# Hybrid trunk kernel: recurrence outputs loaded at the first product of the second double unit, pooled-channel forms tied to places in the product order

## Chip, cores and metric

The kernel runs on one core of one Trainium2 chip, as one launch. The metric is the device time of a launch in microseconds (us).

## What is computed

One layer of a streaming encoder on x of 2048 frames by 1024 channels, in fp32. Two branches read one input projection; each is projected to 1024 channels and merged under sigmoid gates; a gated feed-forward network follows. Cut to what matters here:

```python
xn = rmsnorm(x, norm1_g[l])
z = xn @ w_in[l]
u_pool, zq, zf, zi, zo, zg = jnp.split(z, splits, axis=-1)
gates = jax.nn.sigmoid(zg + b_gate[l]).reshape(B, S, N_BRANCHES, D_MODEL)
ya = pool_mixer(u_pool, pool_w[l], pool_scale[l]) @ w_pa[l]     # pool_mixer: 512 channels
yb = hgrn2_mixer(zq, zf, zi, zo, lower_bounds[l], hgrn_norm_g[l]) @ w_pb[l]   # 4 heads of 128
merged = gates[:, :, 0] * ya + gates[:, :, 1] * yb
x = x + merged @ w_o[l]
x = x + conv_glu_ffn(rmsnorm(x, norm2_g[l]), w_up[l], conv_w[l], conv_b[l], w_down[l])
```

`hgrn2_mixer` is a gated linear recurrence over chunks of frames, with an RMS norm and an output gate behind it; `pool_mixer` subtracts each token from trailing-window means and mixes the channels within four groups.

## The kernel before

**Blocks.** The frames are worked in two blocks of 1024, each of two halves `hf` of 512 (a tile is 128 channels by 512 frames). Names carry the number of the half: `mf0...` is of the first block, `mf2...` of the second.

**Products.** A fp32 operand is split into a high part (a cast on ACT) and a low part (a subtraction on DVE), and each product is three matmuls: high by high, high by low, low by high. `split` does it for activations (L659 ACT, L660 DVE, tiles `...h` and `...l`); the weight stream does it for weights (L231 ACT, L232 DVE, tiles `ops`), which it loads raw on SP's queue (L197, 8 raw buffers and a ring of 6 converted ones). Every matmul of these stages is recorded at L148.

**Units.** The larger projections use a Strassen-Winograd scheme with seven products in the order P1, P6, P5, P7, P2, P4, P3. Each product takes one form of the activations: P1 takes B11, P6 T2, P5 T1, P7 T3, P2 B21, P4 T4 and P3 B22, where T1 to T4 are sums and differences of the quarter blocks. The results go to three banks of PSUM: X (P1, P2), Z (P6, P7, P4) and V (P5, P3). Before a bank is used again, ACT copies X out (`e`, L1200) and DVE combines Z into `u` (L1202 after P6, L1206 after P7), so that P7 waits for the first and P4 for the second.

**Stages of a block's mixer**, in PE's order:
1. the input projections; the last unit is gr_7 (gate channels). The recurrence (pv, po: L1112, L1128, L1130; its transposes pt, L1147) runs among them, and its outputs are stored to memory (`od`) per half and head;
2. pa, the projection of the pooled channels, in two double units (d = 0 is pa_0 and pa_1, d = 1 is pa_2 and pa_3). A product of a double unit is 12 matmuls, and takes one weight. Its results are `ya` (L1161, L1572, L1577, L1579 on DVE, then L1580, the multiplication by the gate `gl`, on POOL);
3. pb, the projection of the recurrence's outputs, 16 chains of 12 matmuls on the split outputs `oTs`;
4. wo, the output projection (`wo_P`), whose forms `yf` are made in pb.

The feed-forward stages come after, with both blocks.

**What sets the order.** The program is written in one order for all engines, and a scheduler moves instructions within an engine's queue by their dependencies and estimated times. Side work is written as generators (`Task`): the kernel counts matmuls, every 6 matmuls are a tick, and at each tick every live task runs to its next `yield n` (n ticks until it goes on). `in_turn(ins)` ties an instruction behind the newest matmul in the scheduler's order; it adds no semaphore.

Two such tasks are touched. `pa_task` fetches the eight pooled tiles (`mx`, L964) at P1 of gr_7 and then makes the forms of pa, one form tile per tick: `minus` (L1486) makes a difference on DVE, L1513 the negated B22 on ACT, and `split` the two parts. Where a product of pa finds its form missing, the loop steps the task until it is there. `halves_task` does the recurrence's outputs from P5 of the second double unit on: it loads one (`oT<-od`, L964, on SP's queue), splits it, waits one tick, and goes to the next. POOL also adds up weights for the stream (L446, tiles `raw` and `w135s`).

Of the kernel before, what the change touches and what calls it, by code (L numbers as in the profile page):

```python
# [14 lines left out]
AF = mybir.ActivationFunctionType  # L15
ALU = mybir.AluOpType
# [6 lines left out]
HEADS = 4  # L23
# [31 lines left out]
PROJ = (("fq", 0), ("g", 0), ("u", 0), ("fq", 1), ("g", 1), ("g", 2), ("fq", 2), ("g", 3),  # L55
        ("u", 1), ("g", 4), ("fq", 3), ("g", 5), ("g", 6), ("g", 7))
# [9 lines left out]
WARM = 24, 5  # L66
GO_IO = (("P2", 1), ("P2", 0))
G_POOL = 4
O_AT, O_LAG = 4, 1
FIN_WAIT = 4  # L70
AHEAD = 3
ADD_LAG = 3
# [9 lines left out]
def tile_trunk(  # L82
# [16 lines left out]
    pe, act, dve, pool, sp = nc.tensor, nc.scalar, nc.vector, nc.gpsimd, nc.sync  # L99
# [9 lines left out]
    def slot(name, cols=TB, dt=F32):  # L109
        return slots.tile([P, cols], dt, tag="s", name=name, padded_shape=[P, 528])  # L110
# [4 lines left out]
    def f32(ap):  # L115
        return ap.bitcast(F32)
# [158 lines left out]
    def in_turn(ins):  # L275

        tc.add_manual_dep(ins.ins, count[1].ins.name, mybir.DependencyInfo(
            mybir.DependencyClass.NoSync, mybir.DependencyReason.SCHED_ONLY), reason="in turn")
# [235 lines left out]
    prep, quiet = [], [False]  # L514
# [136 lines left out]
    last_split = [None]  # L651

    def split(src, name, on_pool=False):
        hi = slot(name + "h", TB, F32R)
        lo = slot(name + "l", TB, F32R)
        if on_pool:
            up = pool.tensor_scalar(hi, src, 1.0, 0.0, ALU.mult, ALU.add)
        else:
            up = act.copy(hi, src)  # L659
        low = dve.tensor_tensor(lo, src, f32(hi), ALU.subtract)  # L660
        last_split[0] = up, low
        return hi, lo
# [299 lines left out]
    def fetch(d, name, eng=sp):  # L962
        t = slot(name)
        eng.dma_start(t, d)  # L964
        return t
# [407 lines left out]
    def mixer(b0, forms, late):  # L1373
# [4 lines left out]
        md, od, gd = {}, {}, {}  # L1378
# [74 lines left out]
                gd[s, m, hf] = spill(t, f"gd{b0 + hf}_{s}_{m}")  # L1453
            return emit

        def halves_task(src, keys, dst, name, lag=1):
            for hf in range(2):
                for g in keys:
                    while (b0 + hf, g) not in src:
                        yield 1  # L1460
                    t = fetch(src[b0 + hf, g], f"{name}{b0 + hf}_{g}")
                    dst[hf, g] = split(t, f"{name}s{b0 + hf}_{g}")
                    yield lag

        gates = {}

        def gate(s, m, hf):
            if (s, m, hf) not in gates:
                gates[s, m, hf] = fetch(gd[s, m, hf], f"gl{b0 + hf}_{s}_{m}")
            return gates[s, m, hf]  # L1470

        pf = {k: [] for k in ("B11", "B21", "B22", "T1", "T2", "T3", "T4")}

        def pa_task():
            t = {}
            for hf, g in ((0, 0), (0, 1), (1, 0), (1, 2), (1, 1), (1, 3), (0, 2), (0, 3)):
                while (b0 + hf, g) not in md:
                    yield 1
                t[hf, g] = fetch(md[b0 + hf, g], f"mx{b0 + hf}_{g}")

            def form(key, j, x):
                pf[key].append(split(x, f"mf{b0}{key}{j}"))

            def minus(key, j, x0, x1, eng=dve):
                x = slot(f"mf{b0}_{key}{j}")
                eng.tensor_tensor(x, x0, x1, ALU.subtract)  # L1486
                return x

            for j in range(2):
                form("B11", j, t[0, j])  # L1490
                yield 1
            t1, t2 = [], []
            for j in range(2):
                t1.append(minus("t1", j, t[1, j], t[0, j]))
                t2.append(minus("t2", j, t[1, j + 2], t1[j]))
                form("T2", j, t2[j])
                yield 1
            t3 = [minus("t3", j, t[1, j], t[1, j + 2], pool) for j in range(2)]
            for j in range(2):
                form("T1", j, t1[j])  # L1500
                yield 1
            for j in range(2):
                form("T3", j, t3[j])
                yield 1
            for j in range(2):
                form("B21", j, t[0, j + 2])
                t4 = minus("t4", j, t[0, j + 2], t2[j])
                yield 1
                form("T4", j, t4)
                yield 1  # L1510
            for j in range(2):
                x = slot(f"mf{b0}_b22{j}")
                act.activation(x, t[1, j + 2], AF.Copy, scale=-1.0)  # L1513
                form("B22", j, x)
                yield 1

        emits = {"fq": emit_fq, "u": emit_u, "g": emit_g}
        oT = {}
        for n, (kind, i) in enumerate(PROJ):
            if (kind, i) == ("u", 0):  # L1520
                held["w"] = stream.get("pw")
            u = Unit(f"{kind[0]}r{b0}_{i}", "in", emits[kind](i))
            for p in ORDER:
                u.multiply(p, forms, late)
                u.after(p)
                if n == len(PROJ) - 1 and p == "P1":
                    quiet[0] = True
                    mtask = Task(pa_task())

        def branch(key, s, xs, evac, each):  # L1530
            ws = {}
# [34 lines left out]
        def emit_a(i):  # L1566
            def emit(s, hf, a, ps):
                m = i + KD // 2 * s
                t = y[m, hf] = slot(f"ya{b0 + hf}_{m}")
                g = gate(0, m, hf)  # L1570
                if a is None:
                    dve.tensor_tensor(t, g, ps, ALU.mult)  # L1572
                    return
                if not hf:
                    value(t, a, ps)
                elif s:
                    dve.scalar_tensor_tensor(t, ps, -1.0, a[0], ALU.mult, ALU.subtract)  # L1577
                else:
                    dve.tensor_tensor(t, ps, a[0], ALU.subtract)  # L1579
                pool.tensor_tensor(t, t, g, ALU.mult)  # L1580
            return emit

        def evac_b(m, hf, g, ps):
            gated(g, hf, g, ps)
            dve.tensor_tensor(y[m, hf], y[m, hf], g, ALU.add)
            if m >= KD // 2 and hf:
                k = m - KD // 2
                two = {(h, r): y[k + r * (KD // 2), h] for h in range(2) for r in range(2)}
                add_forms(two, yf, k, f"yf{b0}", eng=dve)

        otask = []
        for d in range(2):
            units = [Unit(f"pa{b0}_{2 * d + e}", "pa", emit_a(2 * d + e)) for e in range(2)]
            for p in ORDER:
                if (d, p) == (1, "P5"):
                    otask.append(Task(halves_task(od, range(HEADS), oT, "oT", O_LAG)))
                for s_, hf in {"P6": ((1, 1),), "P5": ((0, 0),), "P7": ((1, 0),),
                               "P2": ((0, 1),)}.get(p, ()):
                    for e in range(2):
                        gate(0, 2 * d + e + KD // 2 * s_, hf)  # L1600
                while len(pf[FORM[p]]) < 2:
                    mtask.step()
                w = stream.get("pa")
                for e in range(2):
                    units[e].products(p, pf, pf[FORM[p]], w[:, :, e * 256 : e * 256 + 256])
                    units[e].after(p)
                stream.used(1)
# [340 lines left out]
```

## Time and profile before

| | |
|---|---|
| time, three runs | 2541.48, 2546.94 (median), 2548.03 us |
| profiled execution | 2544.34 us, its span 2542.6 us |
| granted TensorE clock, mean | 0.996 |
| first block, gr_7's first matmul to pa_2's | 419.42 to 474.03 us |
| first block, pa_2's first matmul to wo's | 474.03 to 549.40 us |
| second block, the same two stretches | 1683.32 to 1734.00 and 1734.00 to 1805.46 us |

Times in views are from the start of the span. A row of a timeline has the start, the duration, the engine, the line, the operation, output and inputs; in brackets stands how long the engine had been idle before it and what ended that. A window row has its bounds, its length, the busy time of the engine asked for (and its instructions), the granted clock, the busy share of the DMA engines and GB/s.

### The profile page before, as it was taken

To read this page: it belongs to the slowest core of one execution; us is meant where nothing else is said; L and a number is where in the kernel's file an instruction comes from. 1 tells how busy PE (TensorE), PEld (TensorE's weight loads), DVE (VectorE), ACT (ScalarE), POOL (GpSimd) and SP (SyncE) were. 2 spreads that over 40 slices of the span, in tenths; PEclk is the share of its full clock that TensorE was granted. 3 is DMA by queue.
4 is the path that set the end of the run, shared out by engine and by line. 5 is a ranking of instruction groups with operands and counts; after the bars stand their busy time and mean duration, and the time that the engine had idled before them with its cause. 6 is when DMAs were issued, how large, how long until landed. Compare 5 with 4: busy or idle time off the path is not lost.

```text
span 2542.6 us, 35725 instructions
## 1 busy us (share of the span) xinstructions
PE 2505.1 (99%) x11460; PEld 2049.3 (81%) x11460; DVE 1989.2 (78%) x3528; ACT 1215.1 (48%) x2286; POOL 804.2 (32%) x1171
## 2 busy tenths in 40 slices
PE   9999999899999999999999999998999999999998
PEld 7888888678888888888888888886788888888887
DVE  7787878688999777885596777786979888778755
ACT  6534443325555544554554444543355545445534
POOL 4343453312344334451320202123023432325410
PEclk9999999999999999999999999999999999999999
DMA  8877786587898879997344343446453554446952
GB/s 271 269 199 224 207 227 213 166 256 228 211 250 237 232 230 237 266 363 243 120 150 151 111 130 110 142 137 219 142 166 102 155 153 141 147 140 237 326 164 98
DMA packets 252332, 493.76 MB, mean 194 GB/s; under 512 B 26544, under 2 KB 43056, under 8 KB 251824
## 3 DMA queue, kind: packets, MB, share of 16 engines
q1 hardware_dynamic: 184512, 313.60, 39.0%
q0 software_dynamic: 42656, 112.74, 17.5%
q10 hardware_dynamic: 24976, 65.13, 7.5%
q8 instruction: 91, 1.49, 0.2%
q14 instruction: 97, 0.79, 0.1%
HBM read 381.79 MB, written 187.17 MB: 224 GB/s over the span
## 4 chain that ended last, share of the span: by engine, by line
PE 91%; DVE 3%; DMA 2%; issue 1%; ACT 1%; POOL 1%; SPq 0%; ACTq 0%; POOLq 0%; DVEq 0%
PE dn_P L148 16%; PE up_Z L148 14%; PE up_X L148 10%; PE up_V L148 10%; PE gr_Z L148 5%; PE wo_P L148 5%; PE gr_X L148 3%; PE gr_V L148 3%; PE io_Z L148 3%; PE fr_Z L148 3%; PE pb L148 2%; PE io_V L148 2%; PE fr_V L148 2%; PE fr_X L148 2%; PE pl L1029 2%; PE ur_Z L148 1%
## 5 line engine op out<-in xcount | busy, mean ns | idle before, releaser
L231 ACT CAST ops<-raw 128x512 fp32r<-128x512 f32 x794 | 490.3, 620 | 840.6 <-PE dn_P L148 180.1
L232 DVE TENSOR_TENSOR ops<-raw,ops 128x512 fp32r<-128x512 f32 x794 | 590.5, 747 | 233.8 <-ACT ops L231 228.9
L1681 DVE SCALAR_TENSOR_TENSOR e<-h,cols,e 128x512 f32<-128x512 f32 x176 | 143.3, 818 | 30.5 <-ACT e L1679 23.9
L1679 ACT ACTIVATE e<-h,cols 128x512 f32<-128x512 f32 x176 | 142.2, 814 | 25.3 <-DVE h L1162 18.4
L1684 DVE SCALAR_TENSOR_TENSOR e<-h,cols,e 128x512 f32<-128x512 f32 x176 | 133.9, 770 | 2.5
L964 POOL DMA_DIRECT2D g_P<-dg_P x154 | 83.7, 545 | 160.6 <-PE dn_P L148 111.0
L1275 POOL TENSOR_TENSOR gf_P<-e,e 128x512 f32<-128x512 f32 x44 | 61.1, 1390 | 150.7 <-DVE e L1690 96.1
L446 POOL TENSOR_TENSOR raw<-raw,raw 128x512 f32<-128x512 f32 x36 | 51.2, 1423 | 150.5 <-DVE ops L232 136.5
L1275 POOL TENSOR_TENSOR gf_P<-gf_P,e 128x512 f32<-128x512 f32 x44 | 59.2, 1346 | 71.6 <-DVE e L1690 71.1
L1674 POOL COPY h<-h 128x2 f32<-128x2 f32 x88 | 41.6, 485 | 116.0 <-DVE h L1161 109.2
L1415 POOL TENSOR_TENSOR q<-q,qs 128x512 f32<-128x512 f32 x16 | 21.8, 1362 | 168.6 <-ACT qs L1414 168.6
L1688 ACT ACTIVATE e<-e 128x512 f32<-128x512 f32 x88 | 55.6, 632 | 39.4 <-DVE e L1684 39.0
L1676 POOL COPY hist<-h 128x2 f32<-128x2 f32 x88 | 35.2, 400 | 116.5 <-DVE h L1162 114.7
L1162 DVE TENSOR_TENSOR h<-up_u,up_V 128x512 f32<-128x512 f32 x88 | 60.1, 683 | 10.0 <-PE up_V L148 9.5
L1250 DVE TENSOR_TENSOR x<-x,wo_P 128x512 f32<-128x512 f32 x88 | 55.2, 682 | 8.1 <-PE wo_P L148 8.0
L1452 ACT ACTIVATE gt<-gt,cols 128x512 f32<-128x512 f32 x48 | 34.8, 724 | 53.8 <-DVE gt L1162 44.4
L1250 DVE TENSOR_TENSOR ac<-ac,dn_P 128x512 f32<-128x512 f32 x72 | 47.1, 682 | 16.7 <-PE dn_P L148 16.4
L1014 POOL COPY qm<-q 128x64 f32<-128x64 f32 x64 | 26.6, 439 | 100.8 <-DVE q L1046 20.5
L1580 POOL TENSOR_TENSOR ya<-ya,gl 128x512 f32<-128x512 f32 x24 | 34.2, 1441 | 73.7 <-DVE ya L1161 28.6
L1674 POOL COPY h<-hist 128x2 f32<-128x2 f32 x88 | 44.9, 517 | 27.4 <-DVE m_T42l L660 27.3
L1200 ACT COPY up_e<-up_X 128x512 f32<-128x512 f32 x44 | 25.8, 586 | 57.8 <-PE up_X L148 50.6
L1704 POOL DMA_DIRECT2D dg_P<-gf_P x88 | 50.7, 576 | 8.1 <-POOL gf_P L1275 7.4
(1372 smaller groups left out, 8112.9 us busy)
## 6 DMA issues: line engine op xcount, KB each, us to landing
g_P<-dg_P POOLq DMA_DIRECT2D x154, 256.0 KB, 6.3
raw<-in_w_up_t SPq DMA_DIRECT2D x132, 256.0 KB, 3.3
raw<-in_w_in_t SPq DMA_DIRECT2D x98, 256.0 KB, 3.4
dg_P<-gf_P POOLq DMA_DIRECT2D x88, 256.0 KB, 3.9
dg_P<-e SPq DMA_DIRECT2D x66, 256.0 KB, 3.6
raw<-in_w_dn SPq DMA_DIRECT2D x66, 256.0 KB, 3.6
x<-in_x SPq DMA_DIRECT2D x64, 256.0 KB, 5.3
gd<-gt ACTq DMA_DIRECT2D x64, 256.0 KB, 3.1
```

The source lines that it names most:

```text
L148: count[1] = pe.matmul(*args, **kw)
L231: self.mark = act.copy(hi, v)
L232: low = self.low = dve.tensor_tensor(lo, v, f32(hi), ALU.subtract)
L964: eng.dma_start(t, d)
L1162: return dve.tensor_tensor(dst, t, ps, ALU.add if how == "add" else ALU.subtract)
L1250: dve.tensor_tensor(t, t, ps[j], ALU.add if sg > 0 else ALU.subtract)
L1275: pin(eng.tensor_tensor(t, x0, x1, op))
L1674: pool.tensor_copy(h[:, 0:2], hist[:, mt] if hf == 0 else hs[s, 0][:, TB : TB + 2])
L1679: in_turn(act.activation(t, h[:, 2:], AF.Identity, bias=col(o_cb + mt), scale=col(o_cw + 4 * MF + mt)))
L1681: in_turn(second(dve.scalar_tensor_tensor(t, h[:, 1 : 1 + TB], col(o_cw + 2 * MF + mt), t, ALU.mult, ALU.add)))
L1684: dve.scalar_tensor_tensor(t, h[:, 0:TB], col(o_cw + mt), t, ALU.mult, ALU.add)
L1688: in_turn(act.activation(g, g, AF.Silu))
```

## The change

The change has two parts.

The **recurrence's outputs**: `halves_task` goes, and `o_task` takes its place. It starts at P1 of the second double unit, and not at P5. It fetches all eight tiles in one go, and splits them later, from the time that the counter `place` has reached 17, one every two ticks.

The **pooled forms**: `place` counts the products of gr_7 and of pa (it also goes up each time a product steps the task for a missing form). Each pair of forms now waits for a place: B11 for 3, T2 for 4, T1 and the subtractions of T3 for 6, T3 for 8, B21 for 9, T4 for 10, B22 for 11. gr_7 ends at 7, and P1 of the first double unit is 8. Between the tiles of most pairs two ticks pass in place of one, and the differences, the negations and the splits are tied by `in_turn`.

```diff
--- before.py
+++ after.py
@@ -66,7 +66,7 @@
 WARM = 24, 5
 GO_IO = (("P2", 1), ("P2", 0))
 G_POOL = 4
-O_AT, O_LAG = 4, 1
+O_PLACE = 17
 FIN_WAIT = 4
 AHEAD = 3
 ADD_LAG = 3
@@ -1453,15 +1453,6 @@
                 gd[s, m, hf] = spill(t, f"gd{b0 + hf}_{s}_{m}")
             return emit
 
-        def halves_task(src, keys, dst, name, lag=1):
-            for hf in range(2):
-                for g in keys:
-                    while (b0 + hf, g) not in src:
-                        yield 1
-                    t = fetch(src[b0 + hf, g], f"{name}{b0 + hf}_{g}")
-                    dst[hf, g] = split(t, f"{name}s{b0 + hf}_{g}")
-                    yield lag
-
         gates = {}
 
         def gate(s, m, hf):
@@ -1470,6 +1461,7 @@
             return gates[s, m, hf]
 
         pf = {k: [] for k in ("B11", "B21", "B22", "T1", "T2", "T3", "T4")}
+        place = [0]
 
         def pa_task():
             t = {}
@@ -1480,39 +1472,55 @@
 
             def form(key, j, x):
                 pf[key].append(split(x, f"mf{b0}{key}{j}"))
+                in_turn(last_split[0][0])
 
             def minus(key, j, x0, x1, eng=dve):
                 x = slot(f"mf{b0}_{key}{j}")
-                eng.tensor_tensor(x, x0, x1, ALU.subtract)
+                in_turn(eng.tensor_tensor(x, x0, x1, ALU.subtract))
                 return x
 
+            while place[0] < 3:
+                yield 1
             for j in range(2):
                 form("B11", j, t[0, j])
                 yield 1
             t1, t2 = [], []
+            while place[0] < 4:
+                yield 1
             for j in range(2):
                 t1.append(minus("t1", j, t[1, j], t[0, j]))
                 t2.append(minus("t2", j, t[1, j + 2], t1[j]))
                 form("T2", j, t2[j])
+                yield 2
+            while place[0] < 6:
                 yield 1
             t3 = [minus("t3", j, t[1, j], t[1, j + 2], pool) for j in range(2)]
             for j in range(2):
                 form("T1", j, t1[j])
                 yield 1
+            while place[0] < 8:
+                yield 1
             for j in range(2):
                 form("T3", j, t3[j])
+                yield 2
+            while place[0] < 9:
                 yield 1
             for j in range(2):
                 form("B21", j, t[0, j + 2])
+                yield 2
+            while place[0] < 10:
+                yield 1
+            for j in range(2):
                 t4 = minus("t4", j, t[0, j + 2], t2[j])
-                yield 1
                 form("T4", j, t4)
+                yield 2
+            while place[0] < 11:
                 yield 1
             for j in range(2):
                 x = slot(f"mf{b0}_b22{j}")
-                act.activation(x, t[1, j + 2], AF.Copy, scale=-1.0)
+                in_turn(act.activation(x, t[1, j + 2], AF.Copy, scale=-1.0))
                 form("B22", j, x)
-                yield 1
+                yield 2
 
         emits = {"fq": emit_fq, "u": emit_u, "g": emit_g}
         oT = {}
@@ -1523,9 +1531,11 @@
             for p in ORDER:
                 u.multiply(p, forms, late)
                 u.after(p)
-                if n == len(PROJ) - 1 and p == "P1":
-                    quiet[0] = True
-                    mtask = Task(pa_task())
+                if n == len(PROJ) - 1:
+                    if p == "P1":
+                        quiet[0] = True
+                        mtask = Task(pa_task())
+                    place[0] += 1
 
         def branch(key, s, xs, evac, each):
             ws = {}
@@ -1588,17 +1598,33 @@
                 two = {(h, r): y[k + r * (KD // 2), h] for h in range(2) for r in range(2)}
                 add_forms(two, yf, k, f"yf{b0}", eng=dve)
 
+        def o_task():
+            t = {}
+            for hf in range(2):
+                for g in range(HEADS):
+                    while (b0 + hf, g) not in od:
+                        yield 1
+                    t[hf, g] = fetch(od[b0 + hf, g], f"oT{b0 + hf}_{g}")
+            while place[0] < O_PLACE:
+                yield 1
+            for hf in range(2):
+                for g in range(HEADS):
+                    oT[hf, g] = split(t[hf, g], f"oTs{b0 + hf}_{g}")
+                    yield 2
+
         otask = []
         for d in range(2):
             units = [Unit(f"pa{b0}_{2 * d + e}", "pa", emit_a(2 * d + e)) for e in range(2)]
             for p in ORDER:
-                if (d, p) == (1, "P5"):
-                    otask.append(Task(halves_task(od, range(HEADS), oT, "oT", O_LAG)))
+                place[0] += 1
+                if (d, p) == (1, "P1"):
+                    otask.append(Task(o_task()))
                 for s_, hf in {"P6": ((1, 1),), "P5": ((0, 0),), "P7": ((1, 0),),
                                "P2": ((0, 1),)}.get(p, ()):
                     for e in range(2):
                         gate(0, 2 * d + e + KD // 2 * s_, hf)
                 while len(pf[FORM[p]]) < 2:
+                    place[0] += 1
                     mtask.step()
                 w = stream.get("pa")
                 for e in range(2):
```

DVE's rows at the first double unit of pa in the first block, before: from the second split of T4 to the evacuations of P6 (L1202) and P7 (L1206). `mf0T40l` is the low part of the first T4 tile; `mx_3` is a fetched tile.

```order
L1486 TENSOR_TENSOR mf_t_4844<-mx_3_4635,mf_t_4695 128x512
...
L660 TENSOR_TENSOR mf0T41l<-mf_t_4844,mf0T41h 128x512
L1162 TENSOR_TENSOR gt_0_7_4879<-gr_7_u_4651,gr_7_V 128x512
L232 TENSOR_TENSOR ops_4992<-raw_4560,ops_4992 128x512
L660 TENSOR_TENSOR mf0B220l<-mf_b_4894,mf0B220h 128x512
L660 TENSOR_TENSOR mf0B221l<-mf_b_4909,mf0B221h 128x512
L1202 TENSOR_TENSOR pa_0_u_4933<-pa_0_e_4900,pa_0_Z 128x512
...
L1202 TENSOR_TENSOR pa_1_u_4956<-pa_1_e_4915,pa_1_Z 128x512
L1206 TENSOR_TENSOR pa_0_u_4995<-pa_0_Z,pa_0_e_4900 128x512
```

And of the change, from the evacuation of P7 to the second split of T4:

```order
L1206 TENSOR_TENSOR pa_0_u_4971<-pa_0_Z,pa_0_e_4870 128x512
L1587 SCALAR_TENSOR_TENSOR ya_4_4973<-pa_0_V,pa_0_u_4971 128x512
L1206 TENSOR_TENSOR pa_1_u_4991<-pa_1_Z,pa_1_e_4879 128x512
L1587 SCALAR_TENSOR_TENSOR ya_5_4993<-pa_1_V,pa_1_u_4991 128x512
L1479 TENSOR_TENSOR mf_t_5013<-mx_2_4633,mf_t_4723 128x512
L660 TENSOR_TENSOR mf0T40l<-mf_t_5013,mf0T40h 128x512
L1582 TENSOR_TENSOR ya_0_5019<-gl_0_0_4926,pa_0_X 128x512
L1582 TENSOR_TENSOR ya_1_5027<-gl_0_1_4928,pa_1_X 128x512
L1479 TENSOR_TENSOR mf_t_5029<-mx_3_4635,mf_t_4780 128x512
L232 TENSOR_TENSOR ops_5010<-w135s_5007,ops_5010 128x512
L232 TENSOR_TENSOR ops_5041<-raw_4562,ops_5041 128x512
...
```

All splits of T4 and B22 stood ahead of both evacuations of P6; now they stand behind those of P7, the second T4 split (`mf0T41l`) behind the last row shown and one more weight conversion.

SP's queue at the second double unit of pa, first block, as a piece of the difference (`raw` are weights, `gl` gates, `oT` the recurrence's outputs, `od` where they are stored):

```order
 L197 DMA raw_5077<-in_w_pb_t 128x512
 L197 DMA raw_5079<-in_w_pb_t 128x512
...
-L964 DMA oT_0_5158<-od_0_2304 128x512
-L197 DMA raw_5190<-in_w_o 128x512
-L197 DMA raw_5233<-in_w_o 128x512
-L964 DMA oT_1_5171<-od_1_3085 128x512
...
+L964 DMA oT_0_5103<-od_0_2304 128x512
+L964 DMA oT_1_5105<-od_1_3085 128x512
+L964 DMA oT_2_5107<-od_2_3877 128x512
+L964 DMA oT_3_5109<-od_3_4917 128x512
+L964 DMA oT_0_5111<-od_0_2394 128x512
...
```

The first two loads stood two pb weights, four gates and more behind the pair at the top, with two weights of wo between them; now all eight stand directly behind that pair.

## The prediction

> **What bounds the kernel now.** I read the page first, for the engine that ends the span.
>
> ```profile
> PE 2505.1 (99%) x11460; PEld 2049.3 (81%) x11460; DVE 1989.2 (78%) x3528; ACT 1215.1 (48%) x2286; POOL 804.2 (32%) x1171
> PE 91%; DVE 3%; DMA 2%; issue 1%; ACT 1%; POOL 1%; SPq 0%; ACTq 0%; POOLq 0%; DVEq 0%
> ```
>
> TensorE is the bound: 99% busy, 91% of the chain that ended last. A change that touches no matmul can win only where PE stands idle, or where its clock falls, so the next view is PE's timeline, reduced to the rows with idle time ahead of them, in the stretches that the change touches. Brackets give the idle time and what ended it.
>
> ```profile
> 441.04 0.50 PE L148 MATMUL gr_Z<-x_T40h,ops 128*128 128x512 f32 x1 [1.83 <-DVE gr_u L1206]
> 460.76 0.50 PE L148 MATMUL pa_Z<-mf0T30h,ops 128*128 128x512 f32 x1 [2.49 <-DVE pa_u L1202]
> 495.57 0.85 PE L148 MATMUL pb<-oTs_2h,ops 128*128 128x512 f32 x2 [4.41 <-ACT oTs_2h L659]
> 509.17 0.50 PE L148 MATMUL pb<-oTs_1h,ops 128*128 128x512 f32 x1 [2.43 <-ACT oTs_1h L659]
> 559.15 2.14 PE L148 MATMUL wo_P<-ops,wo_P_3h 128*128 128x512 f32 x8 [1.27 <-ACT wo_P_3h L659]
> ...
> 1704.51 0.50 PE L148 MATMUL gr_Z<-x_T40h,ops 128*128 128x512 f32 x1 [1.83 <-DVE gr_u L1206]
> 1722.30 0.50 PE L148 MATMUL pa_Z<-mf2T30h,ops 128*128 128x512 f32 x1 [1.84 <-DVE pa_u L1202]
> 1752.75 0.73 PE L148 MATMUL pb<-oTs_2h,ops 128*128 128x512 f32 x2 [1.85 <-ACT oTs_2h L659]
> 1765.31 0.50 PE L148 MATMUL pb<-oTs_1h,ops 128*128 128x512 f32 x1 [2.34 <-ACT oTs_1h L659]
> ```
>
> Each block has two kinds of wait. In gr_7 and the first double unit of pa, PE waits for DVE to empty bank Z (gr_u, pa_u). In pb it waits for the split of a recurrence output (oTs). The two columns of times below are the length of a stretch and PE's busy time in it. The first and third rows run from gr_7's first matmul to the first of pa's second double unit (I call this the first half); the second and fourth from there to wo's first (the second half).
>
> ```profile
> 419.42:474.03 54.61, 50.11 (x234) 0.94 0.54 179
> 474.03:549.40 75.37, 68.29 (x278) 0.95 0.69 220
> 1683.32:1734.00 50.68, 47.02 (x234) 1.00 0.54 179
> 1734.00:1805.46 71.46, 66.85 (x278) 0.98 0.64 210
> 474.03:487.89 13.86, 13.86 (x61) 1.00 0.58 195
> 543.61:549.16 5.55, 5.55 (x25) 1.00 0.53 175
> ```
>
> The last two are undisturbed pieces at full clock: five pa products in 13.86 us, 2.772 each, and 24 pb matmuls in 5.55 us, 0.2313 each. Some gaps also cost clock. The number behind the matmul count is the granted clock:
>
> ```profile
> 441.04:444.74 3.70, 3.70 (x10) 0.55 0.18 71
> 509.90:513.05 3.15, 3.15 (x7) 0.50 0.96 363
> 1704.51:1708.00 3.49, 3.49 (x15) 1.00 0.22 80
> ```
>
> The same 1.83 us gap was followed by 3.70 us at 0.55 in the first block, and by full clock in the second. At 0.55, 1.7 us of the 3.70 are lost. So a gap costs its length plus 0 to 1.7 us.
>
> The Trainium skill ("TensorE: Matmul & The Clock Gate", section "Why this matters for your kernels") says that idle gaps of PE above some 3 us bring the slow clock back. By it the waits removed here would cost no clock but for the 4.41 us one, and the sum would be some 3 us smaller. The 0.55 after a 1.83 us gap speaks against it.
>
> **The recurrence's outputs.** These are the queue rows and the landing times of the eight loads in the first block.
>
> ```profile
> 470.60 6.18 SPq L197 DMA_DIRECT2D raw<-in_w_pb_t  x3
> 480.74 0.43 SPq L964 DMA_DIRECT2D oT<-od  x1
> 489.98 0.42 SPq L964 DMA_DIRECT2D oT<-od  x1
> 504.85 0.43 SPq L964 DMA_DIRECT2D oT<-od  x1
> ...
> DMA to landing us min/median/max: 3.6/4.7/6.0
> ...
> L659 ACT CAST oTs_2h<-oT x2: 617/618/619, 494.9 to 512.1; 128x512 fp32r<-128x512 f32 x2
> ...
> SPq L197 <- DVE ops L232: 36.9, 8, 11.6
> ```
>
> The third load leaves at 489.98, lands 4.7 us later (median), is cast in 0.62 us and frees PE at 495.57. The sixth leaves at 504.85, and 3.6 + 0.62 later is the 509.17 row. They leave late because SP's queue holds raw weight loads between them, and those wait for DVE's weight conversions, 36.9 us in all. In the changed order all eight stand together behind the second of a pair of pb weights. That pair waits for the conversions at the end of the first double unit (470.60 here), so by my replay of DVE's order they leave from about 45 us after gr_7's start. Eight at 0.43 us are 3.5 us of queue, with no wait between them; all have landed 50 to 55 us after gr_7's start. PE wants the first 8 us into the second half, about 63. The issue of 3.5 us is queued ahead of the next pb weight; PE then has two conversions in the ring, some 5.5 us of products, so I cost it at nothing; without that cover it is 3.5 us per block. The sixteen splits are the same number as before, earlier; they run where ACT is half idle.
>
> The second half then is 7 x 2.772 = 19.4 and 192 x 0.2313 = 44.4, with 0.7 for the short starts of chains: **64.5 us in both blocks**. The gain is 75.37 - 64.5 = 10.9 and 71.46 - 64.5 = 7.0. This includes the slow clock behind the old gaps, which goes with them.
>
> **The pooled forms.** They are the same casts and subtractions at other places. DVE's rows around the two old waits:
>
> ```profile
> 439.70 0.68 DVE L660 TENSOR_TENSOR mf0T11l<-mf_t,mf0T11h 128x512 fp32r<-128x512 f32 x1
> 440.30 0.68 DVE L1206 TENSOR_TENSOR gr_u<-gr_Z,gr_e 128x512 f32<-128x512 f32 x1
> ...
> 458.43 1.68 DVE L660 TENSOR_TENSOR mf0B221l<-mf_b,mf0B221h 128x512 fp32r<-128x512 f32 x1 [1.36 <-ACT mf0B221h L659]
> 460.04 0.67 DVE L1202 TENSOR_TENSOR pa_u<-pa_e,pa_Z 128x512 f32<-128x512 f32 x1
> ...
> 465.87 0.69 DVE L1206 TENSOR_TENSOR pa_u<-pa_Z,pa_e 128x512 f32<-128x512 f32 x1 [1.66 <-PE pa_Z L148]
> 466.60 0.69 DVE L1577 SCALAR_TENSOR_TENSOR ya<-pa_V,pa_u 128x512 f32<-128x512 f32 x1
> ...
> 468.64 0.69 DVE L1572 TENSOR_TENSOR ya<-gl,pa_X 128x512 f32<-128x512 f32 x1 [0.70 <-PE pa_X L148]
> 469.25 0.69 DVE L232 TENSOR_TENSOR ops<-w135s,ops 128x512 fp32r<-128x512 f32 x1
> ```
>
> Four form splits stood ahead of gr_u; now they come behind it. The splits of T4 and B22 stood ahead of pa_u; now they come behind it by three products. Both old waits go. By DVE's pitch of 0.60 us gr_u is done 14.9 us after gr_7's start, wanted at 18.35, and pa_u 31.8, wanted at 34.4. PE's own work in the first half is the 47.02 us of the second block, which ran at full clock.
>
> What is late next is T4. In the new order DVE reaches its second split (mf0T41l) behind both pa_u, two ya, the first T4 pair, ya of units 0 and 1, a subtraction and three weight conversions. ya of unit 1 waits for the end of P2 of that unit, the last product before P4, so the split cannot be done before PE wants it. From P2's end (40.3 us after gr_7's start) I count ya 0.7, a subtraction 0.6, three conversions 1.8, the split 0.6, and about 1.5 us of waits of the third conversion for its ring buffer: 45.5, wanted at 41.2. **4.3 us**, a new wait. With it B22 is late as well: ACT's cast of the next weight, ahead of its negation, waits for the end of P4; then negation, cast, ya, conversion and split are 1.75 to 3 us. What is queued behind T41l on DVE, ya of P4, B22 and the pb weights, is delayed with it, and that is the same wait, since PE stands still too.
>
> ```profile
> 456.55 3.02 POOL L446 TENSOR_TENSOR raw<-raw,raw 128x512 f32<-128x512 f32 x2 [3.63 <-DVE ops L232]
> 465.53 1.30 POOL L446 TENSOR_TENSOR w135s<-raw,raw 128x512 f32<-128x512 f32 x1
> ...
> 448.00:481.00 33.00, 30.51 (x135) 24.66 (x134) 25.78 (x41) 15.36 (x33) 17.23 (x13) 0.95 0.52 174
> ```
>
> The last row is a stretch of 33 us with the busy time of PE, weight loads, DVE, ACT and POOL in it; DVE has 25.78. The 1.68 us split above (458.43) lay beside the first of these; splits with no POOL work beside them take 0.68. In the new order mf_t, T40l and the conversions lie beside ya and w135s on POOL; with one or two of them held up by 1.0 to 1.6 us the T4 wait is 5.9. Bounds for T4 and B22 together: nothing, if the third conversion finds its buffer free and DVE runs ahead, to 9 us. I take **8 per block**, near the upper end, because the chain from P2's end contains no slack.
>
> The Trainium skill ("SBUF — State Buffer", section "Who interferes with whom") says that a DVE instruction with two SBUF inputs contends with a GpSimd instruction that reads SBUF. This trace agrees, with 1.68 against 0.68 us. The rule speaks against this change: without it the wait would be nearer 6 than 8, and the sum 4 us better.
>
> The first half then takes 47.0 + 8.0 = 55.0: **0.4 more than the 54.61 of the first block, 4.3 more than the 50.68 of the second**. The slow clock behind four new gaps would be 0 to 6.8 us; I take 1, since the new gaps in the second block may be as harmless as that of 1704.51.
>
> **wo.** The forms of yf stand earlier on DVE, which no longer idles through pb; the 1.27 us gap in each block (559.15 above) goes: 2.5 us. It can stay; then it is 0.
>
> **The sum.** 10.9 + 7.0 - 0.4 - 4.3 + 2.5 - 1 = 14.7 us. The profiled execution took 2544.34 us (span 2542.6 and 1.7 around it): 2544.3 - 14.7 = 2529.6, which I call **2530**. That execution lies 2.6 us under the median of the runs, 2546.94, within their spread of 6.5, so I leave that out and let the range hold it.
>
> **Rivals.**
> - The form waits stay small. ya of unit 1 comes only just late and the conversions find their buffers: 0 to 2 us per block in place of 8. Gain 27 to 31, with no slow clock: **2514 to 2518**. For it: DVE was busy only 25.78 of 33 us in this stretch. Against: the wait behind P2 is in the order itself.
> - The form waits are larger. POOL holds up a DVE instruction at each of T4 and B22, and each gap costs clock: 9 per block and 1.7 for each of four gaps, together 8 us worse: **2536 to 2541**.
> - The loads do not come earlier. The changed queue still has a raw pair ahead of them; if that pair waited as the 36.9 us row shows, in the second half, the pb waits stay and the new form waits come on top, 2544.3 + 0.4 + 4.3 - 2.5 = **2547**. Against: the pair ahead is the one that left from 470.60 here, 17 us before the first product of pb (487.89, where the five pa products above end).
> - Slower: a cascade. DVE's queue is in order, and T3, B21, T4, B22 now each stand one to two products ahead of their use. From the point where DVE is some 3.2 us later than I reckon at T3, all four pairs miss, as T4 does, at 4.3 each: 17.2 per block, 9.2 more than taken. The sum is then 14.7 - 18.4 = -3.7, and with 1.7 us of slow clock behind each of eight gaps -3.7 - 13.6 + 1 = -16.3: 2548 without the clock, **2561** with it. For it: in two 1.7 us splits, DVE loses 2 us already in this trace. Against: by my replay B21's split is done 1.5 to 3.5 us before PE wants it.
>
> **How the numbers follow.** A measurement of this kernel tells 0.3%, 7.6 us, from no change: faster is below 2539.3, slower above 2554.6. Forecast (2522 to 2536) 0.50; small waits 0.17; larger waits 0.17; loads not earlier 0.07; cascade 0.09, of which a little falls within 0.3%. Faster 0.50 + 0.17 + 0.14 of the larger waits = 0.81; the same 0.03 + 0.07 + 0.02 = 0.12; slower 0.07. The range of 8 in 10 takes in the forecast, the larger waits and most of the small ones: 2516 to 2541.
>
> **What the changed profile would show.** No idle PE row released by oTs; eight oT loads within 4 us of each other, before pa's second double unit is three products old. The rows gr_Z from x_T40h and pa_Z from T30h without idle time. New rows: pa_Z from a T4 half with 4 to 6 us released by the DVE split of T41l, and pa_V from B22 with 1.75 to 3. The second half 64.5 us in both blocks, the first near 55. The prediction is wrong if T3 or B21 shows a wait, if the T4 row has none, or if a pb weight (ops) takes the place of oTs in the second half.

## The result and the profile after

| | before | after |
|---|---|---|
| median of the runs on one chip | 2544.51 us (4 runs) | 2530.70 us (4 runs, 2528.86 to 2531.84) |
| ratio, 95% interval | | 0.9945 (0.9927 to 0.9962) |
| profiled execution, span | 2544.34, 2542.6 us | 2528.86, 2527.1 us |

The forecast was 2530 us, in a range of 2516 to 2541; the median is 2530.70. The page of the changed kernel: the same engine bounds it, with more of the final chain.

```profile
PE 2503.3 (99%) x11460; PEld 2049.4 (81%) x11460; DVE 1992.4 (79%) x3528; ACT 1215.1 (48%) x2286; POOL 814.2 (32%) x1171
PE 97%; DVE 1%; ACT 1%; DMA 0%; issue 0%; POOL 0%; SPq 0%; DVEq 0%; POOLq 0%; ACTq 0%
```

PE stands at 97% of the chain instead of 91%, although its busy time hardly changed (2505.1 before). PE's timeline of the changed kernel, again only the rows behind idle time; from gr_7 on these are all of them:

```profile
460.14 0.49 PE L148 MATMUL pa_Z<-mf0T40h,ops 128*128 128x512 f32 x1 [0.84 <-ACT mf0T40h L659]
461.17 0.50 PE L148 MATMUL pa_Z<-mf0T40l,ops 128*128 128x512 f32 x1 [0.54 <-DVE mf0T40l L660]
463.62 0.50 PE L148 MATMUL pa_Z<-mf0T41h,ops 128*128 128x512 f32 x1 [1.71 <-ACT mf0T41h L659]
465.38 0.79 PE L148 MATMUL pa_Z<-mf0T41l,ops 128*128 128x512 f32 x1 [1.26 <-DVE mf0T41l L660]
471.05 0.80 PE L148 MATMUL pa_V<-mf0B221h,ops 128*128 128x512 f32 x1 [0.61 <-ACT mf0B221h L659]
472.27 0.80 PE L148 MATMUL pa_V<-mf0B221l,ops 128*128 128x512 f32 x1 [0.42 <-DVE mf0B221l L660]
...
1713.51 0.50 PE L148 MATMUL pa_Z<-mf2T40h,ops 128*128 128x512 f32 x1 [0.86 <-ACT mf2T40h L659]
1714.55 0.50 PE L148 MATMUL pa_Z<-mf2T40l,ops 128*128 128x512 f32 x1 [0.53 <-DVE mf2T40l L660]
1716.99 0.63 PE L148 MATMUL pa_Z<-mf2T41h,ops 128*128 128x512 f32 x1 [1.71 <-ACT mf2T41h L659]
1718.75 0.80 PE L148 MATMUL pa_Z<-mf2T41l,ops 128*128 128x512 f32 x1 [1.13 <-DVE mf2T41l L660]
1724.42 0.50 PE L148 MATMUL pa_V<-mf2B221h,ops 128*128 128x512 f32 x1 [0.61 <-ACT mf2B221h L659]
1725.65 0.50 PE L148 MATMUL pa_V<-mf2B221l,ops 128*128 128x512 f32 x1 [0.72 <-DVE mf2B221l L660]
```

Every wait of before is gone: gr_u, pa_u, oTs and wo_P_3h release no row any more. In their place stand new waits for T4 (4.35 us in the first block, 4.23 in the second) and B22 (1.03 and 1.33). The four stretches, and the pieces behind the T4 waits (length, PE busy, granted clock, DMA share, GB/s):

```profile
418.71:475.36 56.65, 51.27 (x233) 0.91 0.63 210
475.36:539.27 63.91, 63.91 (x277) 1.00 0.75 243
1672.09:1727.61 55.52, 49.96 (x233) 0.94 0.59 203
1727.61:1791.52 63.91, 63.91 (x278) 1.00 0.66 226
465.38:474.90 9.52, 8.48 (x19) 0.51 0.80 273
...
1718.75:1724.40 5.65, 5.06 (x11) 0.53 0.94 324
```

The second halves have no gap at all and full clock. The first halves are longer than before, and behind the T4 waits the clock stays near half, 0.51 and 0.53, for 9.5 and 5.7 us. Put side by side, with the rest of the span between the same first matmuls:

| stretch | before | forecast | after | after - before |
|---|---|---|---|---|
| up to gr_7 of the first block | 419.42 | no change | 418.71 | -0.71 |
| first block, first half | 54.61 | 55.0 | 56.65 | +2.04 |
| first block, second half | 75.37 | 64.5 | 63.91 | -11.46 |
| from wo to gr_7 of the second block | 1133.92 | -1.27 | 1132.82 | -1.10 |
| second block, first half | 50.68 | 55.0 | 55.52 | +4.84 |
| second block, second half | 71.46 | 64.5 | 63.91 | -7.55 |
| from wo to the end | 737.14 | -1.27 | 735.58 | -1.56 |

The sum is -15.5 us, 2542.6 to 2527.1. So one part of the change gives (19.0 us in the second halves, most of 2.7 behind them), the other takes (6.9 us in the first halves).

### The profile page after: what moved, and what is told of

Read it like the earlier page. It is cut to its first block, busy times and chain, and to the rows that moved or that the text cites. A ratio compares the mean times of both kernels' runs of the same rounds, so it can differ in the third digit from the quotient of the medians.

```text
span 2527.1 us, 35765 instructions
## 1 busy us (share of the span) xinstructions
PE 2503.3 (99%) x11460; PEld 2049.4 (81%) x11460; DVE 1992.4 (79%) x3528; ACT 1215.1 (48%) x2286; POOL 814.2 (32%) x1171
## 4 chain that ended last, share of the span: by engine, by line
PE 97%; DVE 1%; ACT 1%; DMA 0%; issue 0%; POOL 0%; SPq 0%; DVEq 0%; POOLq 0%; ACTq 0%
PE dn_P L148 16%; PE up_Z L148 15%; PE up_V L148 10%; PE up_X L148 10%; PE wo_P L148 6%; PE gr_Z L148 5%; PE gr_V L148 4%; PE pb L148 4%; PE gr_X L148 4%; PE io_Z L148 3%; PE fr_Z L148 3%; PE io_V L148 2%; PE fr_V L148 2%; PE fr_X L148 2%; PE pl L1029 2%; PE pa_Z L148 1%
## 5 line engine op out<-in xcount | busy, mean ns | idle before, releaser
L1705 ACT ACTIVATE e<-h,cols 128x512 f32<-128x512 f32 x176 | 142.2, 814 | 25.2 <-DVE h L1162 18.4
```

Source lines behind the costliest of these rows:

```text
L1705: in_turn(act.activation(t, h[:, 2:], AF.Identity, bias=col(o_cb + mt), scale=col(o_cw + 4 * MF + mt)))
```

## The experiments

My theory before the experiments: the two parts act in different stretches and add up. The loads give everything, since they no longer stand between raw weights; the forms, at these places, cost more than they free. The rivals: that the loads need the forms part, or that it is the earlier place of the loads and not the gathering that counts; and, for the forms, that DVE is full and waits only move.

The table has each kernel's stretches, from its own first matmuls; "first" and "second" are the halves, in the first and the second block. Each ratio is against the kernel before on the same chip.

| kernel | median us | ratio (95%) | first | second |
|---|---|---|---|---|
| before | | 1 | 54.61, 50.68 | 75.37, 71.46 |
| the change | 2530.70 | 0.9945 (0.9927 to 0.9962) | 56.65, 55.52 | 63.91, 63.91 |
| e1 loads alone | 2524.19 | 0.9921 (0.9907 to 0.9934) | 50.70, 54.13 | 63.96, 63.88 |
| e2 forms alone | 2555.73 | 1.0049 (1.0035 to 1.0063) | 56.21, 56.99 | 72.48, 73.10 |
| e3 together, at P5 | 2531.35 | 0.9949 (0.9937 to 0.9962) | 57.00, 56.98 | 63.91, 63.95 |
| e4 T4 ahead | 2516.95 | 0.9895 (0.9882 to 0.9909) | 50.69, 49.10 | 63.79, 63.89 |
| e5 T4 and B22 ahead | 2520.23 | 0.9907 (0.9892 to 0.9922) | 50.31, 50.08 | 63.95, 64.02 |
| e6 no gate on POOL | 2528.54 | 0.9940 (0.9925 to 0.9955) | 55.96, 57.04 | 63.85, 64.90 |
| e7 one by one, at P1 | 2549.27 | 1.0023 (1.0013 to 1.0032) | 56.63, 56.97 | 74.11, 73.38 |
| e8 B22 behind ya | 2513.91 | 0.9887 (0.9868 to 0.9905) | 46.75, 46.75 | 64.55, 64.46 |
| e9 as e4, again | 2517.79 | 0.9901 (0.9884 to 0.9917) | 50.78, 50.68 | 64.99, 63.88 |

### e1: the loads alone

`pa_task` is that of before; `o_task` and `place` stay.

```diff
 def form(key, j, x):
     pf[key].append(split(x, f"mf{b0}{key}{j}"))
-    in_turn(last_split[0][0])
...
-while place[0] < 3:
-    yield 1
 for j in range(2):
     form("B11", j, t[0, j])
```

> Only the loads part of the change; the forms are made as before. My theory: the two parts act in different stretches and add up. The second half is 63.9 us in both blocks, as with the whole change, without pb waits and without the 1.27 us wo gaps; the first half goes back to 54.6 and 50.7 (gr_Z 1.83, pa_Z 2.49 and 1.84). The forms part cost 2.0 + 4.8 us there, so the time is 2530.7 - 6.9 = 2523.8. Rival, that the loads need the forms at their new places (DVE's queue gets free earlier, the pair of pb weights ahead of them leaves earlier): pb waits of 2 us or more per block stay, 2530 or above.

Measured 2524.19 us, second halves 63.96 and 63.88. PE's rows behind idle time, from gr_7 to wo, in both blocks:

```profile
440.18 0.50 PE L148 MATMUL gr_Z<-x_T40h,ops 128*128 128x512 f32 x1 [1.83 <-DVE gr_u L1206]
457.94 0.50 PE L148 MATMUL pa_Z<-mf0T30h,ops 128*128 128x512 f32 x1 [1.83 <-DVE pa_u L1202]
1688.58 0.63 PE L148 MATMUL gr_Z<-x_T40h,ops 128*128 128x512 f32 x1 [1.83 <-DVE gr_u L1206]
1708.31 0.50 PE L148 MATMUL pa_Z<-mf2T30h,ops 128*128 128x512 f32 x1 [2.46 <-DVE pa_u L1202]
```

The old first-half waits are back, and neither a pb wait nor a wo wait is. So the loads do not need the forms part. Alone they are some 6 us faster than the whole change by the ratios, whose intervals just overlap (0.9927 to 0.9934). e3, which takes as long as the change, ran on the same chip as e1, and its fastest run, 2528.96 us, is slower than the slowest of e1, 2525.39.

### e2: the forms alone

`o_task` goes, and `halves_task` is back, started at P5.

```diff
-if (d, p) == (1, "P1"):
-    otask.append(Task(o_task()))
+if (d, p) == (1, "P5"):
+    otask.append(Task(halves_task(od, range(HEADS), oT, "oT", 1)))
```

> Only the forms part of the change; the recurrence's outputs are loaded and split one by one from P5 on, as before. My theory: first half 56.7 and 55.5 us (T4 and B22 waits), second half 75.4 and 71.5, wo gaps of 1.27 us stay: 2544.5 + 6.9 = 2551.4. Rival, that the forms part itself takes away pb waits, since DVE has less to do in the second half: second half several us shorter, 2540 to 2546.

Measured 2555.73 us, slower than before. The pb waits of the first block are back, the first of them 2.19 us in place of 4.41 (in the second block it is 2.36, in place of 1.85), and so is the wo wait of 1.27 us in each block:

```profile
495.02 0.74 PE L148 MATMUL pb<-oTs_2h,ops 128*128 128x512 f32 x2 [2.19 <-ACT oTs_2h L659]
507.23 0.49 PE L148 MATMUL pb<-oTs_1h,ops 128*128 128x512 f32 x1 [2.47 <-ACT oTs_1h L659]
```

The rival falls: the forms part takes away none of these waits, though the second half is 2.9 us shorter in the first block (and 1.6 longer in the second). It is 4 us worse than expected; 3.7 us of the 9.9 by which its span exceeds that of before lie behind wo's first matmuls, in stretches that the forms do not touch (one of them a wo wait of 0.59 us that before has not), and I did not follow them further. The two parts, each against before, are -20.1 and +12.5 us by the ratios; together -7.6, and the whole change measured -14. The gap of 6.4 us is hardly more than the intervals allow, which are 3 to 5 us to either side for each of the three. In the stretches where each part acts they do add up: the two second halves together take 127.8 us in e1 and in the change, the two first halves 113.2 in e2 and 112.2 in the change.

### e3 and e7: gathered, or early

e3 is the whole change with the eight loads at P5. e7 has the loads one by one, each with its split, as before, but from P1 on.

```diff
-if (d, p) == (1, "P1"):
+if (d, p) == (1, "P5"):
     otask.append(Task(o_task()))
```

```diff
 if (d, p) == (1, "P1"):
-    otask.append(Task(o_task()))
+    otask.append(Task(halves_task(od, range(HEADS), oT, "oT", 1)))
```

> The whole change, but the eight loads of the recurrence's outputs are written at P5 of the second double unit (as before) instead of P1, all together. Theory that the gathering counts (the loads no longer stand between raw weights that wait for DVE): pb waits of at most 2 us per block, 2531 to 2534. Rival, that the earlier place counts: the first outputs still land too late, pb waits of 4 us and more per block, 2538 to 2542.

> The whole change, but the recurrence's outputs are loaded and split one by one, as before, only from P1 of the second double unit on instead of P5. Theory that the gathering counts and not the place (the loads stand again between raw weights that wait for DVE): pb waits of 2 us and more stay in both blocks, 2535 to 2545. Rival, that either an earlier start or the gathering is enough: no pb wait above 0.5 us, 2530 to 2532.

e3 measured 2531.35 us, the same as the change, and no row in either block waits for oTs. The first fence is SP's queue in e3 at the loads, the second that of the change:

```profile
480.40 0.33 SPq L197 DMA_DIRECT2D raw<-in_w_pb_t  x1
...
481.73 4.77 SPq L964 DMA_DIRECT2D oT<-od  x8
```

```profile
464.18 0.94 SPq L197 DMA_DIRECT2D raw<-in_w_pb_t  x2
465.21 3.72 SPq L964 DMA_DIRECT2D oT<-od  x8
476.94 0.33 SPq L197 DMA_DIRECT2D raw<-in_w_pb_t  x1
```

In e3 the first load leaves at 481.73, no earlier than before the change (480.74), and PE waits for none of the eight. So the 16 us that the change moves the loads forward are worth nothing here; that they stand together is worth the whole gain of the second halves. (e3 also leaves two ticks between the splits where before has one; the runs do not take that apart.)

e7 measured 2549.27 us, slower than before, beyond the 2535 to 2545 of my theory. The largest wait of the first block (the same row of the second waits 6.08 us), and what ACT and DVE did ahead of it:

```profile
503.31 0.80 PE L148 MATMUL pa_Z<-mf0T40h,ops 128*128 128x512 f32 x1 [5.80 <-DVE pa_u L1206]
```

```profile
501.31 0.62 ACT L659 CAST oTs_2h<-oT 128x512 fp32r<-128x512 f32 x1 [2.63 <-DMA oT<-od]
501.96 0.69 DVE L660 TENSOR_TENSOR oTs_2l<-oT,oTs_2h 128x512 fp32r<-128x512 f32 x1 [2.47 <-ACT oTs_2h L659]
502.57 0.68 DVE L1206 TENSOR_TENSOR pa_u<-pa_Z,pa_e 128x512 f32<-128x512 f32 x1
```

The wait changed its name, which neither theory had: with the splits written among pa's products, a split that waits for its late load holds DVE's queue, and behind it stands the evacuation that P4 needs. The pb waits themselves are small in e7 (1.00 and 0.95 us, both for oTs_3). So an earlier start without the gathering loses, in this form, where each split follows its own load. The load of this tile left only at 497.45: the loads still stand between raw weights, which in SP's queue waited 25.2 us for DVE's conversions from 465 to 500 us.

### e4: T4 ahead of the evacuation of P7

B21, T4 and B22 follow at one tick, T4 from place 9, B22 from place 10.

```diff
 for j in range(2):
     form("B21", j, t[0, j + 2])
-    yield 2
-while place[0] < 10:
+    yield 1
+while place[0] < 9:
     yield 1
 for j in range(2):
     t4 = minus("t4", j, t[0, j + 2], t2[j])
     form("T4", j, t4)
-    yield 2
-while place[0] < 11:
+    yield 1
+while place[0] < 10:
     yield 1
...
     form("B22", j, x)
-    yield 2
+    yield 1
```

> The whole change, but the forms B21, T4 and B22 one tick apart and T4 at place 9, B22 at place 10: both splits of T4 now stand on DVE ahead of the evacuation of pa_1's P7 and of ya of P2. My theory (T4 is late because of what stands ahead of it on DVE): the T4 waits of 4.35 and 4.23 us and the slow clock behind them (4.2 and 2.4 us lost) go, B22 keeps 1.0 to 1.3: 2530.7 - 15 = 2515.5, at most 2519. Rival, that the wait only moves: P4 then waits for pa_u behind the T4 splits, or P2 for B21, with the same 4 us per block: 2527 to 2531.

> The same kernel as e4, once more, beside e8 on the same chip: 2516 to 2518, B22 waits of 2.5 us in each block and no T4 wait.

Measured 2516.95 us, and 2517.79 in e9. DVE's rows at the second T4 split, and PE's idle rows from gr_7 to wo in the first block of e4 (the second block has the same two, of 1.40 and 1.13 us):

```profile
458.90 1.02 DVE L660 TENSOR_TENSOR mf0T41l<-mf_t,mf0T41h 128x512 fp32r<-128x512 f32 x1 [0.69 <-ACT mf0T41h L659]
459.84 0.68 DVE L1206 TENSOR_TENSOR pa_u<-pa_Z,pa_e 128x512 f32<-128x512 f32 x1
```

```profile
464.38 0.50 PE L148 MATMUL pa_V<-mf0B221h,ops 128*128 128x512 f32 x1 [1.45 <-ACT mf0B221h L659]
466.02 0.80 PE L148 MATMUL pa_V<-mf0B221l,ops 128*128 128x512 f32 x1 [1.14 <-DVE mf0B221l L660]
```

The T4 waits are gone with nothing in their place at pa_u; B22's grew from 1.0 and 1.3 to 2.6 and 2.5, which my expectation had not. The place in DVE's queue was the cause of the T4 wait: earlier splits end it, although both still take 1.0 us in place of 0.7.

### e5 and e8: B22 too

e5 makes B22 beside B21, ahead of T4, and drops the places of T4 and B22:

```diff
 for j in range(2):
     form("B21", j, t[0, j + 2])
-    yield 2
-while place[0] < 10:
+    x = slot(f"mf{b0}_b22{j}")
+    in_turn(act.activation(x, t[1, j + 2], AF.Copy, scale=-1.0))
+    form("B22", j, x)
     yield 1
 for j in range(2):
     t4 = minus("t4", j, t[0, j + 2], t2[j])
     form("T4", j, t4)
-    yield 2
-while place[0] < 11:
     yield 1
-for j in range(2):
-    x = slot(f"mf{b0}_b22{j}")
...
-    yield 2
```

e8 makes it last, but directly behind T4: the negations beside T4's casts, both splits in the next tick. The places of T4 and B22 go here too, and one tick follows each B21.

```diff
...
+b22 = []
 for j in range(2):
     t4 = minus("t4", j, t[0, j + 2], t2[j])
     form("T4", j, t4)
-    yield 2
-while place[0] < 11:
+    b22.append(slot(f"mf{b0}_b22{j}"))
+    in_turn(act.activation(b22[j], t[1, j + 2], AF.Copy, scale=-1.0))
     yield 1
 for j in range(2):
-    x = slot(f"mf{b0}_b22{j}")
-    in_turn(act.activation(x, t[1, j + 2], AF.Copy, scale=-1.0))
-    form("B22", j, x)
-    yield 2
+    form("B22", j, b22[j])
```

> As e4 (T4 ahead of the evacuation of pa_1's P7), and B22 is made together with B21, ahead of T4. My theory (the form waits that are left come only from the place in the queue): the B22 waits of 2.59 and 2.53 us of e4 and the slow clock behind the first (0.58 for 4 us) go, no idle PE row is left in gr_7 and pa, first half 47.0 to 48 us in both blocks, second 63.9: 2516.9 - 5.1 - 1.5 = 2510.3. Rival, that DVE has no room for both pairs there: pa_u or the P2 operands become late as pa_u was before (1.8 to 2.5 us per block), 2514 to 2518.

> As e4, with B22's negations on ACT beside the T4 casts and both B22 splits made right behind those of T4: on DVE they stand behind the evacuation of pa_1's P7 (unlike e5) and ahead of the weight conversions and ya of P2 (unlike e4). My theory (what counts is that each split stands behind the evacuation that PE wants sooner, and ahead of work that PE wants later): no T4 wait, since nothing is added ahead of pa_1's evacuation, and the B22 waits of 2.5 us of e4 go: first half 47 to 48.5 us in both blocks, 2511 to 2514. Rival, that DVE is simply full in this stretch, so that any order leaves 2 us of waits per block: 2516 to 2520 as e4 and e5.

e5 measured 2520.23 us, above the 2514 to 2518 of its rival, whose mechanism it shows: pa_u is late, and the waits add up to 2.2 and 2.0 us. By the intervals it is not told apart from e4. POOL's and DVE's rows there, and PE's waits in the first block:

```profile
452.82 3.38 POOL L446 TENSOR_TENSOR raw<-raw,raw 128x512 f32<-128x512 f32 x2 [4.65 <-DVE ops L232]
453.63 1.41 DVE L660 TENSOR_TENSOR mf0B220l<-mf_b,mf0B220h 128x512 fp32r<-128x512 f32 x1 [0.30 <-ACT mf0B220h L659]
454.97 1.77 DVE L660 TENSOR_TENSOR mf0B211l<-mx,mf0B211h 128x512 fp32r<-128x512 f32 x1
...
459.25 0.68 DVE L1206 TENSOR_TENSOR pa_u<-pa_Z,pa_e 128x512 f32<-128x512 f32 x1
```

```profile
460.08 0.47 PE L148 MATMUL pa_Z<-mf0T40h,ops 128*128 128x512 f32 x1 [0.73 <-DVE pa_u L1206]
461.96 0.50 PE L148 MATMUL pa_Z<-mf0T41h,ops 128*128 128x512 f32 x1 [0.95 <-ACT mf0T41h L659]
462.99 0.79 PE L148 MATMUL pa_Z<-mf0T41l,ops 128*128 128x512 f32 x1 [0.54 <-DVE mf0T41l L660]
```

B22 no longer waits, but the splits of B22 and B21 ahead of T4, beside two POOL sums of weights, take 1.4 and 1.8 us instead of 0.7, and push pa_u and T4. So it is the added splits and POOL's hold on them together; the runs do not part the two.

The waits of e8 in the first block (0.45 and 0.51 us at the same rows of the second):

```profile
463.15 0.50 PE L148 MATMUL pa_V<-mf0B221l,ops 128*128 128x512 f32 x1 [0.45 <-DVE mf0B221l L660]
474.06 0.50 PE L148 MATMUL pa_Z<-mf0T30h,ops 128*128 128x512 f32 x1 [0.48 <-DVE pa_u L1202]
```

e8 measured 2513.91 us, in its expected 2511 to 2514: first halves of 46.75 us in both blocks, with one wait of 0.45 us for B22 in each; the second halves are 0.6 us longer, with one wait of 0.5 us for pa_u. That DVE is simply full falls by the waits, 0.9 to 1.0 us per block against the 2 of the rival; the order decides. By its interval (0.9868 to 0.9905) e8 is faster than the change and than before; against e9 on the same chip the intervals overlap, and I do not call it faster than that.

### e6: POOL beside DVE

The multiplication by the gate on POOL in pa is left out, so `ya` of these products lacks its gate; all else is the whole change.

```diff
-pool.tensor_tensor(t, t, g, ALU.mult)
 return emit
```

> The whole change without the multiplication of ya by the gate on POOL in pa (the gate is left out of ya of these products). Theory that part of the T4 wait is POOL holding up DVE: the subtraction of the first T4 tile takes 0.68 us in place of 1.56 and 1.58, the splits of T40 0.7 in place of 1.0, and the T4 waits of 4.35 and 4.23 us fall by about 0.9 each, to 3.4; time 2528 to 2529. Rival, that POOL plays no part: the subtraction stays at 1.5 us and the waits at 4.2 to 4.4.

Of the change, DVE's subtraction for T4 and what POOL did beside it; then e6, both blocks:

```profile
457.59 1.30 POOL L446 TENSOR_TENSOR w135s<-raw,raw 128x512 f32<-128x512 f32 x1
457.88 1.56 DVE L1479 TENSOR_TENSOR mf_t<-mx,mf_t 128x512 f32<-128x512 f32 x1
...
460.12 0.99 DVE L660 TENSOR_TENSOR mf0T40l<-mf_t,mf0T40h 128x512 fp32r<-128x512 f32 x1 [0.69 <-ACT mf0T40h L659]
```

```profile
456.27 1.30 POOL L446 TENSOR_TENSOR w135s<-raw,raw 128x512 f32<-128x512 f32 x1
...
457.79 0.68 DVE L1479 TENSOR_TENSOR mf_t<-mx,mf_t 128x512 f32<-128x512 f32 x1
...
1710.11 1.30 POOL L446 TENSOR_TENSOR w543s<-raw,raw 128x512 f32<-128x512 f32 x1
...
1710.55 1.41 DVE L1479 TENSOR_TENSOR mf_t<-mx,mf_t 128x512 f32<-128x512 f32 x1
```

Without the gate, w135s ran earlier in the first block and the subtraction took 0.68; the T4 wait fell from 4.35 to 3.20 (0.23, 1.71 and 1.26). In the second block a POOL sum still lay beside it, the subtraction took 1.41, and the wait fell only from 4.23 to 3.93. So about 0.7 us (3.93 less 3.20) to 1.1 us of the T4 wait is POOL's hold on DVE; the larger part is the queue. The block as a whole gains little by it: in the first block the B22 wait grew from 1.03 to 2.21, with its last split at 1.48 us beside another POOL sum, so that the two waits together are 5.41 us against 5.38 (5.24 against 5.56 in the second). The time, 2528.54, was in the expected range, and by the intervals it is not told apart from the change.

## Why the prediction was right

By the spans the forecast gain of 14.7 us was 15.5. The second halves gave 1.1 us more than forecast, and the first halves cost 1.2 more. The first of these terms was right by its mechanism; the second is close by luck, as the terms below show.

**The second halves**, forecast at 64.5 us, measured 63.91 twice. The step held: the waits were the queue's, not the DMA's, and the slow clock went with them. The eight loads left 46.5 us after gr_7's start (465.21 - 418.71; forecast about 45), in 3.72 us (forecast 3.5), and the next pb weight behind them cost nothing. What the prediction left open, whether the earlier place or the gathering does it, e3 and e7 settle.

**The rival "loads not earlier"** did not come about, and e3 shows that its conclusion did not follow from its condition: there the first load leaves 6 us into the second half, no earlier than before, and the full gain of the second halves is there.

**The old form waits** went, as forecast, and T3 and B21 had none: no cascade.

**The T4 wait** was forecast at 4.3 us (5.9 with POOL's hold) and measured 4.35 and 4.23. That the size agrees is luck, for the working was not right. I had the second split alone late, through ya's wait for the end of P2 and a wait of conversions for the ring. DVE's rows show neither wait: no idle time stands ahead of them (conversions left out where the dots are).

```profile
461.04 1.27 DVE L1582 TENSOR_TENSOR ya<-gl,pa_X 128x512 f32<-128x512 f32 x2
...
464.64 0.68 DVE L660 TENSOR_TENSOR mf0T41l<-mf_t,mf0T41h 128x512 fp32r<-128x512 f32 x1
```

The first T4 tile is late already (0.84 + 0.54), its subtraction held by POOL, and the second follows by the mere length of the queue. Of the 4 to 6 us that the row of T41l was to show, it shows 1.26; 1.71 stand at the cast T41h, which waits for its subtraction on DVE. POOL's hold, priced at 1.6 us, was there and was worth about 1.1 in the first block: without the gate on POOL the wait is 3.20 (e6), not 4.3.

The Trainium skill ("SBUF — State Buffer", section "Who interferes with whom") has a DVE instruction with two SBUF inputs contend with a GpSimd instruction that reads SBUF; 0.68 against 1.41 to 1.58 in e6 and the change agrees. DVE is not always the one that is held: in e4 three DVE rows from 452.69 to 453.90 took 0.69 each, and the two POOL sums beside them 4.58 us, against 1.30 for a single one in e6 (at 456.27). The 4 us in the sum that the prediction hung on POOL's hold did not show: with the gate gone (the sums of weights stay on POOL) the waits for T4 and B22 are 5.41 and 5.24 us, against 5.38 and 5.56.

**B22** with T4 was taken at 8 us per block and measured 5.38 and 5.56: B22 is 1.0 and 1.3, under the 1.75 to 3 of my chain.

**The slow clock** was taken at 1 us in all. With the prediction's 47.0 us of PE work the first halves leave 56.65 - 47.0 - 5.38 = 4.3 and 55.52 - 47.0 - 5.56 = 3.0, 7.3 in all (somewhat more by e8, whose 46.75 contain a wait of 0.45). The two pieces behind the T4 waits alone lose about 6.6 by my estimate: their 19 and 11 matmuls took 8.48 and 5.06 us, against 0.2313 us each at full clock. This term was mis-sized: it lies at the 6.8 us that I gave as its upper bound or above. I priced a gap at no more than the 3.70 us at 0.55 behind one old gap and took most new gaps as harmless; behind the four gaps of T4 the clock stayed low for 9.5 and 5.7 us, in both blocks. By chance it offsets the 5.1 us too much in the waits: 17 us taken, 18.2 measured. The forecast owes its closeness largely to that.

**The sums.** One rival is added up wrongly: small form waits would give 2513 to 2517 by its own terms (16 or 12 us less wait and 1 us less slow clock), not 2514 to 2518. It changes nothing in the forecast.

**wo**: forecast 2.5 us, the two gaps of 1.27 are gone, and the two stretches that hold them are 2.7 shorter. e1 has no such gap and e2 has both, so they go with the loads part.

## What to carry to other kernels

Where a queue that works in order holds loads between transfers that wait for another engine, write the loads that are needed together as one group: in this kernel their place mattered less than what stands between them. Tie side work not to "late enough" but to its two neighbours in the queue: behind the evacuation that is wanted sooner, ahead of the work that is wanted later. And take a bundled change apart, for one half may pay for the other.

## What the runs showed of the hardware

The clock after a gap of PE did not go by the gap alone. In the profiles of before, e1 and e2, four gaps of 1.27 us were all followed by full clock; seven of 1.83 to 1.85 us by full clock five times and by 0.55 twice, in the same place of the program in different blocks or runs; eight of 2.19 to 2.49 us by 0.50 to 0.67 seven times and by full clock once (the clock is the mean of the 3 to 5 us behind the gap). Two rows of e1 show it:

```profile
440.18:444.00 3.82, 3.82 (x17) 1.00 0.18 69
...
1688.58:1692.40 3.82, 3.82 (x10) 0.55 0.20 73
```

Behind the same wait of 1.83 us PE ran 17 matmuls in 3.82 us once, and 10 in the same time once. Four short waits within about 6 us (the T4 rows, 4.35 and 4.23 us in all) were followed by a clock of 0.51 and 0.53 for 9.5 and 5.7 us in the two blocks of the change. What decides in one case and not in the other stays open.

The Trainium skill ("TensorE: Matmul & The Clock Gate", section "Why this matters for your kernels") puts the gap from which the clock falls at about 3 us; here gaps of 1.83 to 2.49 us were enough in nine of fifteen cases, and the measurement decides.
